# Delta net: the triangular solve by substitution on blocks of 16 rows, joined to 32 by products on quarters of the array

## The chip, the cores and the metric

The kernel runs on one core of a Trainium2 chip. It is one launch; the metric is the device time of that launch in microseconds. The engines in the profile are PE (TensorE matmuls), PEld (its weight loads), DVE (VectorE), ACT (ScalarE), POOL (GpSimd) and SP (SyncE, which here issues DMAs).

## The reference

A trunk of two layers on 1024 positions of 1024 channels. Layer 0 mixes with a gated delta net of eight heads, layer 1 with a retention; each has a convolutional FFN behind it. The change is inside the delta net. Cut to what matters:

```python
def gated_deltanet(h, w_in, conv_w, a_log, dt_bias, norm_w, w_out):
    ...
    kk = jnp.where(strict, jnp.einsum('bhncd,bhnmd->bhncm', kb, k) * decay, 0.0)
    eye = jnp.eye(C, dtype=F32)
    rhs = jnp.concatenate([v * beta[..., None], kb * jnp.exp(gc)[..., None]], axis=-1)
    sol = lax.linalg.triangular_solve(kk + eye, rhs, left_side=True, lower=True, unit_diagonal=True)
    u, w = sol[..., :dv], sol[..., dv:]
    ...
    def step(state, inp):
        q_n, k_n, u_n, w_n, qk_n, g_n = inp
        v_new = u_n - jnp.einsum('bhck,bhkv->bhcv', w_n, state)
        o = (jnp.einsum('bhck,bhkv->bhcv', q_n * jnp.exp(g_n)[..., None], state)
             + jnp.einsum('bhcm,bhmv->bhcv', qk_n, v_new))
        ...
```

Per head and chunk there is a unit lower triangular matrix, the identity plus the strictly lower part of the decayed key products. The kernel forms its inverse, here called T, and multiplies by it.

## The kernel before, in words

The kernel uses chunks of 128 positions (`P`), so eight chunks (`NCH`) for each of the eight heads (`GH`). It works on heads in pairs p = 0 to 3 and solves in two quads: `t_solve(0)` for pairs 0 and 1, `t_solve(1)` for pairs 2 and 3. The delta-net stage is one call, `run(todo)`, and stands at about 91 to 646 us of the profiled execution.

`run` interleaves generators ("streams"). Each stream has a priority, and each `yield` says after what planned delay, or after which events, it may go on. A planned clock `clk` advances by the cost given with every TensorE instruction (`pm` L630, a product; `ptr` L633, a transpose), and `pq` pins TensorE's order to the order in which the streams issue. So the planner's numbers (`cost`, the table `LAT`) fix TensorE's order; they are not the times of the chip. The order on the other engines is set by a scheduler when the kernel is built. The lowest priority belongs to `filler`: 24 items of projections for later heads and eight of the gate `z`, each of 48 products 512 wide (`acc<-hT,wh` and `acc<-hT,wl`, "fills" below). After an item, `filler` may run up to two background steps (`bg_step`, whose loads are `mvw` and whose VectorE instructions are L223 among others), but none while the list `busy` holds something.

The streams that touch the change, in the order of one pair:

- `t_front(p)`: decay factors into `U[h]` (a head's 128x128 blocks for the eight chunks), a copy of them to DRAM (`Ld`), then the key products `kk` in PSUM, multiplied into `U` (L776). The next quad's front waits for the event `Tq` of the solve before it.
- `t_solve(qd)`: copies the 32x32 diagonal blocks of 32 matrices (four heads, eight chunks) to X (L788), transposes them on VectorE to Y (L792), and builds T by 31 substitution steps: a multiply to `fs` (L800) and a subtract in T (L802), in which 128 partitions hold (block, matrix) and the free axis holds rows by columns, 31 to 256 elements. RX is T transposed back (L806); TP is a permuted copy (L808), TX its transpose (L810): both orientations of the inverted 32x32 blocks. Then `busy` is cleared and `Tq` and `T` are told.
- `t_chain(p)`: copies TX and RX to T0 and R (L838, L849, L851) and joins blocks of 32 to 64 and of 64 to 128 by small products (U on T0, the result `xa`, then `xa` and R).
- `prep(p)` (L914: values; also the keys) and `dt_half(p, q4)`: load a decay half from `Ld` to a tile DT (L941), form the scores in PSUM and multiply them into DT (L949). Both wait for `Tq`.
- `scan(p, h)`: the recurrence over the eight chunks.

SBUF tiles come from tagged pools; a new tile of a tag waits for the readers of the one whose place it takes. "lane" has four places (X, Y, T, RX, TP, TX, T0 and one DT), "t2" three. PSUM tiles of `mm` have two places, `acc` four, `sc` two.

## Time and profile before

| | |
|---|---|
| median of 3 runs | 2946.01 us (2941.49 to 2947.28) |
| the profiled execution | 2946.19 us, span 2944.4 us, mean granted TensorE clock 0.986 |
| PE, PEld, DVE, ACT, POOL busy | 96%, 78%, 75%, 45%, 20% of the span |
| delta-net stage, 91 to 646 us | 555 us: PE 520.32, DVE 384.64, ACT 302.27, POOL 120.62 us busy |

How to read the lines that follow: a group has the source line, engine, operation, out<-in by the program's names, shape and count, then busy us and mean ns of one, then idle time of the engine just before it. A row of a timeline has the start and length in us; the bracket holds the idle time ahead of it and what ended that. A window has its start and end, its length, then busy us and counts of PE, PEld, DVE, ACT and POOL, the granted clock, the DMA share and GB/s. Line numbers are those of the kernel before; in the changed kernel they move (the product is L634, the transpose L637, the substitution L813 and L816, the multiply into DT L990, the one in `prep` L955).

### The profile page before, as it was taken

The numbers are of one execution on the slowest core, as the hardware profiler recorded it, in microseconds if no ns is written. First come the engines' busy times: TensorE is split into PE (matmuls) and PEld (weight loads), VectorE is DVE, ScalarE is ACT, GpSimd is POOL, SyncE is SP. The second block draws the span as 40 slices with busy tenths as digits, with TensorE's granted clock in tenths as the row PEclk, the third lists the DMA queues.
The fourth block names the chain that finished last, engine by engine and source line by source line (L and its number), as shares of the span: only waits on it lengthen the run. The fifth ranks groups of instructions, "written<-read, shape, count | busy, mean of one in ns | idle before, by whom it ended". The sixth has DMA issues, their size and how long they took to land. (4 is left out here: it accounts for less than half of the span.)

```text
span 2944.4 us, 38880 instructions
## 1 busy us (share of the span) xinstructions
PE 2817.4 (96%) x13638; PEld 2300.7 (78%) x13638; DVE 2212.1 (75%) x3869; ACT 1317.5 (45%) x2457; POOL 580.1 (20%) x613
## 2 busy tenths in 40 slices
PE   8998999999999999999999999999999899999997
PEld 7787877887778888777787877777778688888786
DVE  5695687556788888987677766666697887778989
ACT  3655455443544444536543333221345544445443
POOL 0311220134011111520023300322201011112601
PEclk9999999999999999999999999999999999999999
DMA  8122321354344544864434454555664243335653
GB/s 300 71 79 73 104 84 50 105 181 149 111 149 159 164 157 149 306 205 139 146 119 161 157 177 153 165 172 154 197 232 152 96 136 108 108 108 197 240 179 122
DMA packets 237188, 442.36 MB, mean 150 GB/s; under 512 B 22848, under 2 KB 76352, under 8 KB 236992
## 3 DMA queue, kind: packets, MB, share of 16 engines
q1 hardware_dynamic: 206832, 387.96, 39.3%
q10 hardware_dynamic: 25152, 34.61, 3.2%
q0 software_dynamic: 5008, 17.30, 1.5%
q8 instruction: 107, 1.75, 0.2%
q14 instruction: 89, 0.73, 0.1%
HBM read 331.26 MB, written 108.53 MB: 149 GB/s over the span
## 5 line engine op out<-in xcount | busy, mean ns | idle before, releaser
L1466 PE MATMUL acc<-bb,ab 128*128 128x512 f32 x1800 | 430.5, 393 | 7.5 <-DVE bb L90 3.7
L1466 PEld LDWEIGHTS acc<-bb,ab 128*128 128x128 f32 x1800 | 338.9, 189 | 82.6 <-DVE bb L90 6.0
L630 PE MATMUL acc<-hT,wh 128*128 128x512 f32 x960 | 300.9, 395 | 0.0
L1603 POOL TENSOR_TENSOR o<-o 128x512 f32<-128x512 f32 x88 | 118.8, 1360 | 721.1 <-DVE o L1596 685.5
L1159 PE MATMUL acc<-T,wb 128*128 128x512 f32 x840 | 204.6, 393 | 7.2 <-DVE wb L90 7.2
L630 PEld LDWEIGHTS acc<-hT,wh 128*128 128x128 f32 x960 | 183.5, 191 | 34.4
L630 PE MATMUL acc<-hT,wl 128*128 128x512 f32 x480 | 203.5, 424 | 0.5 <-ACT ada L235 0.3
L89 ACT ACTIVATE ab<-ar 128x512 fp32r<-128x512 f32 x210 | 129.5, 624 | 165.2 <-PE acc L1466 89.0
L1159 PEld LDWEIGHTS acc<-T,wb 128*128 128x128 f32 x840 | 157.7, 189 | 44.3 <-DVE wb L90 11.6
L90 DVE TENSOR_TENSOR ab<-ar,ab 128x512 fp32r<-128x512 f32 x210 | 168.2, 806 | 29.6 <-ACT ab L89 29.2
L90 DVE TENSOR_TENSOR wb<-wr,wb 128x512 fp32r<-128x512 f32 x162 | 119.1, 736 | 65.7 <-ACT wb L89 65.3
L90 DVE TENSOR_TENSOR wb<-mm,wb 128x512 fp32r<-128x512 f32 x216 | 144.9, 684 | 21.5 <-ACT wb L89 19.5
L89 ACT ACTIVATE wh<-wr 128x1024 fp32r<-128x1024 f32 x101 | 107.0, 1061 | 115.0 <-PE acc L630 56.4
L90 DVE TENSOR_TENSOR wl<-wr,wh 128x1024 fp32r<-128x1024 f32 x85 | 105.2, 1237 | 66.2 <-ACT wh L89 64.0
L89 ACT ACTIVATE wb<-mm 128x512 fp32r<-128x512 f32 x216 | 122.3, 593 | 71.1 <-DVE mm L1205 70.5
L1225 ACT ACTIVATE pc<-acc 128x512 f32<-128x512 f32 x143 | 84.7, 592 | 152.7 <-PE acc L1159 99.8
L89 ACT ACTIVATE wb<-wr 128x512 fp32r<-128x512 f32 x162 | 99.4, 626 | 96.3 <-DMA wr<-in_ffn_up 53.4
L449 DVE SCALAR_TENSOR_TENSOR qkv<-raw,vc,qkv 128x512 f32<-128x512 f32 x144 | 112.2, 783 | 35.4 <-ACT qkv L447 33.2
L630 PE MATMUL acc<-wh,hT 128*128 128x512 f32 x384 | 136.0, 417 | 0.7 <-DVE vv L90 0.6
L1582 DVE SCALAR_TENSOR_TENSOR o<-g,vc,o 128x512 f32<-128x512 f32 (+2 forms) x176 | 135.3, 787 | 0.9 <-ACT o L1577 0.2
L223 DVE SCALAR_TENSOR_TENSOR ada<-mvw,e,ada 128x512 f32<-128x512 f32 x140 | 107.0, 764 | 27.3 <-DMA mvw<-in_ada_w 26.9
L110 PE MATMUL acc<-T,wb 128*128 128x512 f32 x292 | 116.7, 400 | 10.4 <-DVE wb L90 9.9
(628 smaller groups left out, 7023.9 us busy)
## 6 DMA issues: line engine op xcount, KB each, us to landing
wr<-in_ffn_up SPq DMA_DIRECT2D x96, 512.0 KB, 4.3
ad<-o SPq DMA_DIRECT2D x154, 256.0 KB, 2.3
ar<-ad SPq DMA_DIRECT2D x154, 256.0 KB, 3.8
mvw<-in_ada_w SPq DMA_DIRECT2D x48, 512.0 KB, 6.5
Br<-in_ffn_down SPq DMA_DIRECT2D x66, 256.0 KB, 3.7
mvw<-in_ada_w SPq DMA_DIRECT2D x64, 256.0 KB, 3.0
wr<-in_ret_wv SPq DMA_DIRECT2D x32, 512.0 KB, 4.1
ar<-od SPq DMA_DIRECT2D x56, 256.0 KB, 4.8
```

The lines of the kernel that those rows point to most:

```text
L89: act.activation(dst_h, src, AF.Copy)
L90: eng.tensor_tensor(dst_l, src, dst_h, ALU.subtract)
L110: mm(acc, wl[:, k], hl[0], start=first, stop=False)
L223: dve.scalar_tensor_tensor(a, wr[kk], e[:, k:k + 1], a, ALU.mult, ALU.add)
L449: dve.scalar_tensor_tensor(oh, raw[:, 3 - j:515 - j], w[:, 3 - j:4 - j], oh, ALU.mult, ALU.add)
L630: pq(pe.matmul(out, lhsT, rhs, start=start, stop=stop, **kw), cost)
L1159: return pe.matmul(*a, skip_group_check=True, **kw)
L1225: act.activation(t, X, AF.Copy)
L1466: mm_ = (lambda *a, p=p, onto=onto, **kw: (mm if p < 2 else pe.matmul)(*a, skip_group_check=onto, **kw))
L1582: dve.scalar_tensor_tensor(tv, gv[:, c0 - j:c1 - j], w[:, 2 - j:3 - j], tv, ALU.mult, ALU.add)
L1603: pool.tensor_tensor(o[d], o[x], o[y], op)
```

## The change

The substitution runs on blocks of 16 rows, two for each 32x32 block, in the same free axis: 15 steps in place of 31. Two mask columns are made at setup: m0 is 1 on the first 16 partitions of each 32, m1 on the other 16. X is folded so that each partition keeps the half of the columns that belongs to its own 16-row block. After the substitution the two inverted 16-blocks are transposed in both orientations as halves, and four masked copies put them into RX and TX as block diagonals. The off-diagonal 16-block is then made by TensorE for each matrix and each of the four 32-row blocks: `pa` is U times TX's left half, `xa` its masked copy, `pn` and `pt` are the products of `xa` with RX in the two orientations, subtracted into TX and RX. `busy.clear()` and the event `Tq` stand ahead of the joins; `T` behind them. 384 products per solve are added, 768 in all.

```diff
+    m0, m1 = mhalf[:, 4:5], mhalf[:, 5:6]
+    part = tl("sm", [P, NCH], name="part")
+    dve.tensor_reduce(part, ident.rearrange("p (x r) -> p x r", r=16), AX.X, ALU.add)
+    dve.tensor_reduce(mhalf[:, 4:6], part.rearrange("p (b s) -> p s b", s=2), AX.X, ALU.add)
...
-        Y = tl("lane", [P, 32, 32], name="Y")
-        dve.transpose(flat(Y), flat(X))
-        T = tl("lane", [P, 32, 32], name="T")
+        XY = tl("lane", [P, 2, 16, 32], name="Y")
+        act.activation(XY[:, 0], X[:, 0:16], AF.Copy, scale=m0)
+        dve.scalar_tensor_tensor(XY[:, 0], X[:, 16:32], m1, XY[:, 0], ALU.mult, ALU.add)
+        Y = XY[:, 1]
+        dve.transpose(flat(Y), flat(XY[:, 0]))
+        Y = Y.rearrange("p i (s r) -> p i s r", s=2)
+        TT = tl("lane", [P, 2, 16, 32], name="T")
+        T = TT[:, 0]
         pool.memset(T, 0.0)
-        pool.memset(flat(T)[:, 0:1024:33], 1.0)
+        for s2 in (0, 16):
+            pool.memset(flat(T)[:, s2:512:33], 1.0)
+        Tv = T.rearrange("p i (s j) -> p i s j", s=2)
         tmp = tl("fs", [P, 256], name="fs")
-        for j in range(31):
-            ni, nj = 31 - j, j + 1
-            tv = tmp[:, 0:ni * nj].rearrange("p (i j) -> p i j", j=nj)
-            dve.tensor_tensor(tv, bc(Y[:, j + 1:, j], nj), bm(T[:, j, 0:nj], ni), ALU.mult)
-            ts_ = T[:, j + 1:, 0:nj]
+        for j in range(15):
+            ni, nj = 15 - j, j + 1
+            shape = [P, ni, 2, nj]
+            tv = tmp[:, 0:2 * ni * nj].rearrange("p (i s j) -> p i s j", s=2, j=nj)
+            dve.tensor_tensor(tv, Y[:, j + 1:, :, j].unsqueeze(3).to_broadcast(shape),
+                              Tv[:, j, :, 0:nj].unsqueeze(1).to_broadcast(shape), ALU.mult)
+            ts_ = Tv[:, j + 1:, :, 0:nj]
             dve.tensor_tensor(ts_, ts_, tv, ALU.subtract)
             if j % 2:
                 yield LAT["fs"]
+        busy.clear()
+        emit(("Tq", qd_))
+        half = tl("lane", [P, 2, 16, 32], name="RTh")
+        dve.transpose(flat(half[:, 0]), flat(T))
+        act.activation(TT[:, 1].rearrange("p j (s i) -> p j s i", s=2), Tv.rearrange("p i s j -> p j s i"), AF.Copy)
+        dve.transpose(flat(half[:, 1]), flat(TT[:, 1]))
         RX = tl("lane", [P, 32, 32], name="RX")
-        dve.transpose(flat(RX), flat(T))
-        TP = tl("lane", [P, 32, 32], name="TP")
-        act.activation(TP, T.rearrange("p i j -> p j i"), AF.Copy)
         TX = tl("lane", [P, 32, 32], name="TX")
-        dve.transpose(flat(TX), flat(TP))
+        for t, c in ((RX, half[:, 0]), (TX, half[:, 1])):
+            for g, m in ((slice(0, 16), m0), (slice(16, 32), m1)):
+                act.activation(t[:, g], c, AF.Copy, scale=m)
+        xa = tl("lane", [P, 32, 32], name="xa")
+        pool.memset(xa, 0.0)
+        yield LAT["h1"]
...
+        pa = mm_tile()
+        for c, h, n in lists:
+            for bs in quads:
+                pm(pa[bs, cols(c)], U[h][bs, n, bs], TX[bs, 0:16, c], cost=0.016)
+        act.activation(xa[:, :, 0:16], pa.rearrange("p (c j) -> p c j", j=16), AF.Copy, scale=m1)
+        yield LAT["h2"]
+        pn, pt = mm_tile(), mm_tile()
+        for c, h, n in lists:
+            for bs in quads:
+                pm(pn[bs, cols(c)], RX[bs, :, c], xa[bs, c, 0:16], cost=0.016)
+        for c, h, n in lists:
+            for bs in quads:
+                pm(pt[bs, cols(c)], xa[bs, c], RX[bs, 16:32, c], cost=0.016)
+        for t, pb in ((TX[:, 0:16], pn), (RX[:, 16:32], pt)):
+            dve.tensor_tensor(t, t, pb.rearrange("p (c j) -> p j c", j=16), ALU.subtract)
         RTX[qd_] = (RX, TX)
         give("lane", 1)
-        busy.clear()
-        emit(("Tq", qd_))
         emit(("T", qd_), LAT["T"])
...
-    LAT = {... "T": 4.98, ... "fs": 2.2, ...}
+    LAT = {... "T": 2.6, ... "fs": 1.6, "h1": 5.0, "h2": 1.8, ...}
```

The change also moves work. On TensorE, from the first score product of `dt_half` at the end of solve 1 (`mm<-qkv,qkv`: scores; `mm<-cst,qkv`: transposes of `prep`; `acc<-hT`: fills), before:

```order
L630 MATMUL mm_1890<-qkv_1339,qkv_685 128x128 x4
L630 MATMUL mm_1896<-qkv_1394,qkv_686 128x128 x4
L633 MATMUL mm_1902<-cst_155,qkv_1143 128x128 x4
L633 MATMUL mm_1908<-cst_155,qkv_1703 128x128 x4
L630 MATMUL acc_1850<-hT_491,wl_1847 128x512
L630 MATMUL acc_1850<-hT_491,wh_1846 128x512 x2
L630 MATMUL mm_1917<-qkv_1479,qkv_695 128x128 x4
L630 MATMUL mm_1956<-qkv_1543,qkv_696 128x128 x4
```

And after, where the first `pa` group (TX on U) follows:

```order
L634 MATMUL mm_1682<-qkv_1342,qkv_685 128x128 x4
L634 MATMUL mm_1688<-qkv_1397,qkv_686 128x128 x4
L637 MATMUL mm_1694<-cst_155,qkv_1146 128x128 x4
L634 MATMUL acc_1610<-hT_658,wl_1565 128x512
L634 MATMUL acc_1610<-hT_658,wh_1564 128x512 x2
L634 MATMUL mm_1703<-qkv_1485,qkv_695 128x128 x4
L634 MATMUL mm_1709<-qkv_1553,qkv_696 128x128 x4
L637 MATMUL mm_1715<-cst_155,qkv_1059 128x128 x4
L634 MATMUL mm_1721<-TX_1634,U_889 32x16 x32
L634 MATMUL mm_1721<-TX_1634,U_954 32x16 x32
```

The score products stand in the same order. Between the last common pair of transposes (those of `ssq`, two groups ahead) and the first score product stand 48 + 108 + 3 = 159 fills before and 39 + 6 = 45 now: 114 fewer.

On VectorE at the end of solve 1, before:

```order
L802 TENSOR_TENSOR T_1471<-T_1471,fs_1474 128x31
L806 STREAM_TRANSPOSE RX_1862<-T_1471 128x1024
L810 STREAM_TRANSPOSE TX_1866<-TP_1864 128x1024
L949 TENSOR_TENSOR DT_1868<-DT_1868,mm_1890 128x512
L949 TENSOR_TENSOR DT_1868<-DT_1868,mm_1917 128x512
L949 TENSOR_TENSOR DT_1872<-DT_1872,mm_1956 128x512
```

And after:

```order
L990 TENSOR_TENSOR DT_1644<-DT_1644,mm_1688 128x512
...
L816 TENSOR_TENSOR T_1476<-T_1476,fs_1480 128x2x15
L822 STREAM_TRANSPOSE RTh_1629<-T_1476 128x512
L824 STREAM_TRANSPOSE RTh_1629<-T_1476 128x512
L990 TENSOR_TENSOR DT_1641<-DT_1641,mm_1682 128x512
L990 TENSOR_TENSOR DT_1641<-DT_1641,mm_1703 128x512
L990 TENSOR_TENSOR DT_1645<-DT_1645,mm_1709 128x512
```

The reader of mm_1682 stands behind the substitution and both transposes, as its like did before; it needs the load of DT_1641, which takes a lane place.

On VectorE at the end of solve 2, before (L914 readies keys and values):

```order
L802 TENSOR_TENSOR T_4014<-T_4014,fs_4017 128x31
L949 TENSOR_TENSOR DT_4401<-DT_4401,mm_4423 128x512
L806 STREAM_TRANSPOSE RX_4392<-T_4014 128x1024
L914 TENSOR_TENSOR qkv_3996<-mm_4429,ir_3671 128x512
L810 STREAM_TRANSPOSE TX_4396<-TP_4394 128x1024
L949 TENSOR_TENSOR DT_4398<-DT_4398,mm_4417 128x512
```

And after:

```order
L955 TENSOR_TENSOR qkv_4155<-mm_4445,ir_3827 128x512
L824 STREAM_TRANSPOSE RTh_4356<-T_4222 128x512
L260 TENSOR_TENSOR fh01_6897<-fh01_6897,v03_3582 128x8
L223 SCALAR_TENSOR_TENSOR ada_4422<-mvw_4424,e_162,ada_4422 128x512
L223 SCALAR_TENSOR_TENSOR ada_4422<-mvw_5008,e_162,ada_4422 128x512
L223 SCALAR_TENSOR_TENSOR ada_4422<-mvw_5009,e_162,ada_4422 128x512
L223 SCALAR_TENSOR_TENSOR ada_4422<-mvw_5269,e_162,ada_4422 128x512
L223 SCALAR_TENSOR_TENSOR ada_4422<-mvw_5270,e_162,ada_4422 128x512
L223 SCALAR_TENSOR_TENSOR ada_4422<-mvw_5426,e_162,ada_4422 128x512
L223 SCALAR_TENSOR_TENSOR ada_4422<-mvw_5427,e_162,ada_4422 128x512
L955 TENSOR_TENSOR qkv_4273<-mm_4581,ir_3945 128x512
L853 TENSOR_TENSOR TX_4361<-TX_4361,mm_4596 128x512
```

Seven L223 of a background step, with the loads of `mvw`, now stand between the last half transpose of solve 2 and its joins (L853).

More of the change, by code (lines that the diff above doesn't have):

```diff
@@ L783, in t_solve @@
         busy.append(qd_)
+        heads = pairs[2 * qd_] + pairs[2 * qd_ + 1]
         X = tl("lane", [P, 32, 32], name="X")
-        for h in pairs[2 * qd_] + pairs[2 * qd_ + 1]:
+        for h in heads:
             for b in range(4):
@@ L804, in t_solve, with cols @@
                 yield LAT["fs"]
+        busy.clear()
[4 more added lines that the diff above has]
+        dve.transpose(flat(half[:, 1]), flat(TT[:, 1]))
         RX = tl("lane", [P, 32, 32], name="RX")
-        dve.transpose(flat(RX), flat(T))
-        TP = tl("lane", [P, 32, 32], name="TP")
-        act.activation(TP, T.rearrange("p i j -> p j i"), AF.Copy)
         TX = tl("lane", [P, 32, 32], name="TX")
-        dve.transpose(flat(TX), flat(TP))
+        for t, c in ((RX, half[:, 0]), (TX, half[:, 1])):
[4 more added lines that the diff above has]
+        yield LAT["h1"]
+        quads = [slice(32 * b, 32 * b + 32) for b in range(4)]
+        lists = [(h % 4 * 8 + n, h, n) for h in heads for n in range(NCH)]
+        def cols(c):
+            return slice(16 * c, 16 * c + 16)
+        pa = mm_tile()
[13 more added lines that the diff above has]
+            dve.tensor_tensor(t, t, pb.rearrange("p (c j) -> p j c", j=16), ALU.subtract)
         RTX[qd_] = (RX, TX)
         give("lane", 1)
-        busy.clear()
-        emit(("Tq", qd_))
         emit(("T", qd_), LAT["T"])
@@ L1092, in filler @@
                 owed[0] -= 1
-    LAT = {"kk": 3.05, "ld": 1.14, "g1": 17.30, "gm": 2.50, "mm": 1.81, "T": 4.98, "X": 3.38, "fs": 2.2, "T0": 5.00, "t1": 1.65, "t2": 2.35, "t3": 1.34, "D": 2.67, "s1": 1.60, "s2": 1.22, "s3": 1.26, "tail": 12.31, "ssq": 9.30, "fv": 2.85}
+    LAT = {"kk": 3.05, "ld": 1.14, "g1": 17.30, "gm": 2.50, "mm": 1.81, "T": 2.6, "X": 3.38, "fs": 1.6, "h1": 5.0, "h2": 1.8, "T0": 5.00, "t1": 1.65, "t2": 2.35, "t3": 1.34, "D": 2.67, "s1": 1.60, "s2": 1.22, "s3": 1.26, "tail": 12.31, "ssq": 9.30, "fv": 2.85}
     pairs = [(2 * p, 2 * p + 1) for p in range(GH // 2)]
```

## The prediction

> **What bounds the kernel now.** I read the page's busy shares first, then the windows of the delta-net stage (91 to 646 us; only it is touched), the waits of TensorE in it, and the timelines at its stalls. The page:

> ```profile
> PE 2817.4 (96%) x13638; PEld 2300.7 (78%) x13638; DVE 2212.1 (75%) x3869; ACT 1317.5 (45%) x2457; POOL 580.1 (20%) x613
> ```

> TensorE is busy 96% of the span. The windows (start:end, length; then busy us and count of PE, PEld, DVE, ACT, POOL; granted clock, DMA share, GB/s):

> ```profile
> 143.00:174.00 31.00, 31.00 (x163) 26.37 (x162) 27.50 (x110) 24.54 (x42) 6.91 (x10) 1.00 0.19 65
> 174.00:216.00 42.00, 41.45 (x195) 34.22 (x194) 39.17 (x83) 21.30 (x59) 0.94 (x7) 1.00 0.23 79
> 216.00:236.00 20.00, 11.76 (x65) 10.17 (x66) 13.40 (x29) 12.52 (x29) 5.25 (x15) 0.83 0.15 52
> 385.00:412.00 27.00, 20.58 (x107) 16.80 (x106) 23.82 (x103) 16.89 (x30) 8.49 (x13) 0.89 0.39 136
> 412.00:478.00 66.00, 65.41 (x313) 54.62 (x312) 58.20 (x144) 35.03 (x80) 5.70 (x14) 1.00 0.15 54
> 478.00:486.00 8.00, 4.87 (x28) 4.21 (x29) 5.18 (x7) 7.82 (x16) 5.25 (x14) 0.89 0.33 122
> 560.00:646.00 86.00, 86.00 (x558) 75.92 (x559) 47.20 (x111) 36.19 (x83) 18.61 (x13) 0.98 0.44 154
> ```

> The substitutions run in 174:216 and 412:478. There TensorE is full (41.45 of 42, 65.41 of 66) with the filler's projections, while VectorE is nearly full too. And 560:646 is 86.00 of 86.00: the stage ends in projections that fill every gap. So a projection pulled forward into a hole shortens the tail, one pushed back lengthens it, and the stage's time is TensorE's work plus its waits. A shorter substitution by itself buys nothing; it counts only through the waits. These are (us in total, times, longest):

> ```profile
> PE mm L630 <- DVE DT L949: 8.1, 2, 5.6
> PE mm L630 <- DVE U L776: 4.1, 1, 4.1
> PE acc L327 <- DVE hl L90: 2.8, 1, 2.8
> ```

> The stalls sit at the end of solve 1 (216:236: 8.2 us idle and, at a clock of 0.83, 3.4 us lost to speed: 11.6), at the end of solve 2 (478:486: 3.1 + 0.9 = 4.0) and in the `kk` products of pairs 2 and 3 (385:412: 6.4 + 3.0 = 9.4).

> **Part 1: 768 small products (+13.0).** Each solve adds three groups of 128 products on 32x16 or 32x32 quarters. The nearest rows are the 32x32 joins of `t_chain` (a group by form: count, then busy us; and two rows of one pair's `pb`; each fp32 product leaves two records):

> ```profile
> L630 PE MATMUL mm<-T,U 32*32 32x32 f32 x256 | 8.4, 192 | 0.0
> 242.38 0.21 PE L630 MATMUL mm<-R,xa 32*32 32x32 f32 x1
> 243.41 1.08 PE L630 MATMUL mm<-R,xa 32*32 32x32 f32 x29
> ```

> T,U: 128 products, each on the same quarter of the array as the one before it, in 8.4 us: 66 ns each. From 242.38 to 243.41 R,xa and xa,R alternate between two column quarters, 32 products in 1.03 us: 32 ns; the 16 that follow sit on one quarter again and take 1.08. The new groups go round four diagonal quarters. Two quarters halved the time, so I take four to quarter it: 16 ns, an estimate. 768 x 0.016 = 12.3 us, plus six group changes of 0.1 to 0.2 us, 0.7. Ends: 6.5 if the 16-wide operand halves it once more, and 51 at 66 ns.

> The rows show two column quarters of one PSUM bank written together; none shows two row quarters doing so. [...]

> **Part 2: the substitution on VectorE (0 by itself).** Rows:

> ```profile
> L802 DVE TENSOR_TENSOR T<-T,fs 128x31 f32<-128x31 f32 (+15 forms) x62 | 21.1, 340 | 1.2
> L800 DVE TENSOR_TENSOR fs<-Y,T 128x31 f32<-128x31 f32 (+15 forms) x62 | 21.1, 340 | 1.1
> 435.55 0.25 DVE L800 TENSOR_TENSOR fs<-Y,T 128x87 f32<-128x87 f32 x1
> ```

> 42.2 us become 60 instructions of 30 to 128 elements, on average 91, so 60 x 0.25 = 15 us: 27 us fall off VectorE. The 1024-wide transposes (1.25 us each) become three halves, and a 0.75 us fold is added. ScalarE's added masks (about 5 us a solve) and GpSimd's memset lie beside a full TensorE except at the solve's end, below. [...]

> **Part 3: the end of solve 1 (+1.7).** Here is what stands there before:

> ```profile
> 173.30 1.25 DVE L792 STREAM_TRANSPOSE Y<-X 128x1024 f32<-128x1024 f32 x1 [0.44 <-ACT X L788]
> 216.96 2.05 PE L630 MATMUL mm<-qkv 128*128 128x128 f32 x16 [1.51 <-DVE qkv L914]
> 219.80 0.66 PE L633 MATMUL mm<-cst,qkv 128*128 128x128 f32 x4 [0.79 <-DVE DT L949]
> 221.30 0.66 PE L633 MATMUL mm<-cst,qkv 128*128 128x128 f32 x4 [0.85 <-DVE qkv L914]
> 223.84 1.96 ACT L808 ACTIVATE TP<-T 128x1024 f32<-128x1024 f32 x1 [5.01 <-DVE T L802]
> 228.71 1.42 DVE L949 TENSOR_TENSOR DT<-DT,mm 128x512 f32<-128x512 f32 x2 [1.63 <-DMA DT<-Ld]
> 229.45 2.08 PE L630 MATMUL mm<-qkv 128*128 128x128 f32 x8 [5.56 <-DVE DT L949]
> 398.45 1.06 PE L630 MATMUL mm<-qkv 128*128 128x128 f32 x8
> ...
> 168.83 0.39 PE L630 MATMUL acc<-hT,wh 128*128 128x512 f32 x1
> 169.06 0.39 PE L630 MATMUL acc<-hT,wl 128*128 128x512 f32 x1
> 169.28 0.62 PE L630 MATMUL acc<-hT,wh 128*128 128x512 f32 x2
> 169.74 0.39 PE L630 MATMUL acc<-hT,wl 128*128 128x512 f32 x1
> ```

> TensorE reaches the score products of `dt_half`, and waits 1.51 + 0.79 + 0.85 + 5.56 = 8.7 us. The last is a chain: T ready 223.8, `TP` copied to 225.8, the load of `DT` (it takes a lane buffer that `TP`'s reader frees) lands 2.9 us later at 228.7, and the multiply releases a PSUM buffer. Afterwards eight records take 2.08 us in place of 1.06 (the row at 398.45): half speed.

> After the change, Tq comes ahead of the joins, and in the new order 114 fewer projections stand ahead of the first score product. At 0.227 us each (three from 169.06 to 169.74) TensorE gets there 25.8 us sooner than 216.96 - 1.51 = 215.45, at 189.6, and is past the first two scores (1.06 us) near 190.9. VectorE begins at 173.3 with the fold (0.6 + 0.75) and half transpose (0.65), then 30 substitution steps with their gaps (8.7), and by the new order 7 of L449 (0.746), 3 of L223 (0.75, and their loads some 1.6), one L90 (1.2), two L955, one L990 (0.69 each) and two small ones: 12.4 in all, so T is ready near 197. Half transposes and the masks of L829 (0.65 + 0.6 + 0.65 + half of 2.4) put TX at 200.4. The load for DT_1641 now waits for RTh's readers, the masks, so it lands 2.9 later, 203.3; its multiply releases mm_1709 at 204, where TensorE arrives near 195.9. `mm` has two PSUM buffers; mm_1682 holds one, and mm_1694 and mm_1703 each wait for the reader of the other, an L990 and an L955 among the substitution's rows, 2.4 us. With the 8.1 for mm_1709 that is 10.5 against 8.7, with the same half-speed stretch. **+1.7**; between -8.7 (the load finds its buffer early) and +5 (VectorE 3 us later).

> **Part 4: the end of solve 2 (+5.5).** Before:

> ```profile
> L449 DVE SCALAR_TENSOR_TENSOR qkv<-raw,vc,qkv 128x512 f32<-128x512 f32 x28 | 20.9, 746 | 1.6 <-ACT qkv L447 1.5
> 423.99 1.05 PE L630 MATMUL mm<-qkv 128*128 128x128 f32 x8
> 482.89 1.49 DVE L949 TENSOR_TENSOR DT<-DT,mm 128x512 f32<-128x512 f32 x2 [1.62 <-DMA DT<-Ld]
> 483.64 1.50 PE L630 MATMUL mm<-qkv 128*128 128x128 f32 x8 [2.56 <-DVE DT L949]
> ```

> Count from the last `kk` product (423.99). The new order puts 114 projections and a few transposes ahead of the first `pa` product, so TensorE is there after 28.7 us. VectorE starts the solve after 8.5 us and has in its order, up to the second half transpose (L824), 7.5 + 0.9 us of substitution, 17 of L449, and L90 and L955 rows: 24.4 us, so it ends at 33.0 and TX follows at 33.6. TensorE waits 5 us and then pays a half-speed stretch of 2.6 (five us at half speed, as after 407 and 229). Next, `pt` needs a PSUM buffer whose reader (L955 on mm_4581) stands behind seven L223 and their three successive loads; at some 3.7 us a pair that ends at 45.2, with `pn` done at 43: 2 more. 9.6 against 4.0, **+5.5**; between -4 (no wait) and +9.

> **Part 5: the `kk` stage (-6.5).** The `busy` list now empties earlier in solve 1 and later background steps are taken elsewhere: the new order has no L223 between the `kk` products of pairs 2 and 3. Before:

> ```profile
> L223 DVE SCALAR_TENSOR_TENSOR ada<-mvw,e,ada 128x512 f32<-128x512 f32 x5 | 3.7, 747 | 0.4 <-DMA mvw<-in_ada_w 0.4
> 407.29 2.08 PE L630 MATMUL mm<-qkv 128*128 128x128 f32 x8 [4.10 <-DVE U L776]
> ```

> VectorE is 23.82 of 27 busy there and TensorE waits for its L776. With 3.7 us less ahead, most of the 4.1 us wait and its half-speed stretch (2.6) go: -6.5 of the 9.4. Ends: 0 and -9.4.

> **Part 6: the stage's end (-1.5).** The tail now ends in more projections, so the first product behind it (L327) may find its operand ready: half of 2.8. What the scans wait for (Sn L985 and the like) keeps its order: 0, +-3. The two reductions at setup: 0, hidden by TensorE's first projections; 0.5 if not.

> **Sum.** +13.0 + 1.7 + 5.5 - 6.5 - 1.5 = +12.2 on the profiled execution's 2946.19 (span 2944.4 and 1.8 outside it), 0.2 above the median of 2946.01: 2958.

> **Rivals.**

> *A, the four quarters run in series.* 66 ns each: 768 x 0.066 = 50.7 in place of 12.3, +38.4: 2997. For it: nothing shown has two row quarters at work in one bank. Against: column quarters of one bank do overlap. 10 in 100.

> *B, only two quarters overlap.* 32 ns as in the R,xa row: +12.3, 2971. For it: it is the only overlap the trace has. 13 in 100.

> *C, faster: VectorE, 27 us lighter, is ahead of TensorE at both solves.* Its place is the PSUM and lane buffers at mm_1709 and TX at `pa`: if DT's load is out before TensorE's 195.9, and TX ready before 28.7, the waits of Parts 3 and 4 vanish with their slow stretches (-11.6 and -4.0) and Parts 1 and 5 leave +6.5: less Part 6, 13.0 - 11.6 - 4.0 - 6.5 - 1.5 = -10.6, 2935. It decides at 5 us on VectorE in solve 2 and 8 in solve 1. For it: VectorE's lighter load is the larger number. Against: the orders keep VectorE at the solve's end full with L449, and the chain of masks and load is longer, not shorter. 17 in 100.

> *D, no change.* Solve 2's joins find TX ready (-9.6 on my sum): 2949. 17 in 100.

> **Numbers.** Mine has the remaining 43; its own range is 2952 to 2966. 0.2% (5.9 us) is about what a measurement can tell from no change. Slower: mine, A and B, 66; same: D, 17; faster: C, 17. The range of 2936 to 2974 leaves out A and half of C.

> **What would show it.** Each of the six groups `pa`, `pn`, `pt` is about 2 us wide (A: 8.4; B: 4.1). TensorE's waits list an 8 us one on L990 near 204 and a 5 us one on TX (ACT L829) in solve 2, then one on L955 behind L223. 385:412 loses under 4 us. L813 and L816 sum to about 15 us. I am wrong if the groups are wider than 3 us each, or if the two stalls at the solves are shorter than those before.

## The result, and the profile after

The changed kernel takes 2988.36 us (median of 4 runs, 2984.91 to 2989.87) against 2943.75 us for the kernel before on the same chip: a ratio of 1.0147, 95% interval 1.0134 to 1.0159. It is slower by 43 us by the ratio (44.6 between the two medians), where +12 was forecast with 2974 as the upper end. The profiled execution took 2987.05 us (span 2985.3).

The page of the changed kernel, busy shares and one line of its DMA queues, and behind it the same DMA line of the kernel before:

```profile
PE 2843.7 (95%) x15174; PEld 2325.4 (78%) x15174; DVE 2175.2 (73%) x3813; ACT 1325.5 (44%) x2471; POOL 582.0 (19%) x617
q8 instruction: 119, 1.95, 0.3%
```

```profile
q8 instruction: 107, 1.75, 0.2%
```

TensorE has 1536 more matmuls, two for each of the 768 products, and as many more weight loads: 3072 instructions. VectorE has lost 37 us. The second line counts a queue of loads that neither kernel issues, the instructions themselves: packets, MB, share of the DMA engines. 12 more packets came, 0.0164 MB each, one for each 256 of the added instructions.

The windows of the changed kernel, at the stretches shown of the kernel before and at two more:

```profile
143.00:174.00 31.00, 31.00 (x164) 26.32 (x162) 28.47 (x110) 23.76 (x42) 6.41 (x9) 1.00 0.26 86
174.00:216.00 42.00, 30.16 (x588) 25.56 (x589) 25.28 (x59) 16.10 (x50) 2.10 (x4) 0.84 0.19 54
216.00:236.00 20.00, 17.11 (x412) 14.59 (x407) 2.87 (x4) 10.55 (x20) 5.71 (x16) 0.74 0.06 23
236.00:300.00 64.00, 56.73 (x415) 47.41 (x412) 38.18 (x81) 30.56 (x78) 5.02 (x12) 0.89 0.21 67
385.00:412.00 27.00, 25.11 (x132) 20.59 (x131) 24.60 (x68) 18.31 (x27) 13.72 (x16) 1.00 0.36 125
412.00:478.00 66.00, 53.41 (x879) 45.31 (x880) 48.69 (x155) 30.55 (x52) 7.30 (x12) 0.88 0.23 73
478.00:486.00 8.00, 8.00 (x146) 7.38 (x143) 0.69 (x1) 6.17 (x13) 5.50 (x15) 0.69 0.02 4
```

Look at the clock column: 0.84, 0.74, 0.89, 0.88, 0.69 around both solves. Before, 174:216, 236:300 and 412:478 stood at 1.00, and 216:236 and 478:486 at 0.83 and 0.89. In 478:486 TensorE is busy throughout and still at two thirds of its speed. From the first solve on the stage runs some 14 us later than before, so 385:412 now holds only the first part of the `kk` products; Part 5 below comes back to that.

To divide the loss I took windows of 1 us from 91 us to the stage's end (the first product of L327, at 649.36 before and 693.87 after): idle is their length less PE's busy time, the loss to speed is busy time times one minus the clock. Idle went from 37.5 to 52.2 us (+14.7), the loss to speed from 12.3 to 27.9 (+15.6), and the rest of the 44.5 us, 14.2, is work. (The split between the last two is rough: the burst of `pt` at 218.16, shown below, ran at 0.50 and took 1.90 of the 3.46 us to the next one, so the low clock there need not have cost time.) Of the waits of TensorE in the stage after the change, these bear on the argument:

```profile
PE mm L634 <- issue: 10.7, 6, 2.7
PE mm L634 <- DVE DT L990: 8.4, 2, 8.0
PE mm L634 <- ACT TX L829: 4.4, 1, 4.4
PE mm L634 <- DVE R L923: 3.3, 1, 3.3
```

The second and third were forecast. The first was not: "issue" is time in which TensorE waited for nothing that the profile shows, and all six cases are inside the new groups. The timeline at the end of solve 1:

```profile
199.65 2.08 PE L634 MATMUL mm<-qkv 128*128 128x128 f32 x8 [7.97 <-DVE DT L990]
201.52 1.06 PE L637 MATMUL mm<-cst,qkv 128*128 128x128 f32 x4
202.60 1.56 PE L634 MATMUL mm<-TX,U 32*32 32x16 f32 x149
206.43 1.67 PE L634 MATMUL mm<-TX,U 32*32 32x16 f32 x107 [2.26 <-issue]
...
212.92 3.82 PE L634 MATMUL mm<-xa,RX 32*32 32x16 f32 x256
216.58 0.25 PE L634 MATMUL mm<-RX,xa 32*32 32x16 f32 x8
218.16 1.90 PE L634 MATMUL mm<-RX,xa 32*32 32x16 f32 x128 [1.34 <-issue]
221.62 1.80 PE L634 MATMUL mm<-RX,xa 32*32 32x16 f32 x120 [1.55 <-issue]
```

`pa` breaks off after 149 records, `pt` runs in a burst of exactly 128 and waits again. 128 matmuls and their 128 weight loads are 256 instructions, and 218.16 to 221.62 is 3.46 us. At 17 ns a product (measured in e1 below) the 64 products of such a burst would be done in 1.1 us.

The queue of instructions shows the supply itself. Here is the DMA rate of the changed kernel from 200 to 225 us, in 40 slices of 0.625 us, and the count of that queue's packets:

```profile
GB/s 0 0 0 0 0 0 26 0 0 0 0 0 26 0 0 0 0 0 26 0 0 0 0 0 105 170 334 223 26 7 26 0 0 0 0 0 26 0 0 0
q8 instruction: 6, 0.10, 1.7%
```

The values of 26 in the slices from 203.75, 207.5, 211.25, 218.75 and 222.5 are one packet of 16 KB each; a sixth, at 215.46, lies under another load. Those that start at 203.79, 215.46 and 219.20 land at 205.00, 216.64 and 220.20, and the bursts at 206.43, 218.16 and 221.62 begin 1.4 to 1.5 us behind them. It is the same at all 49 holes of this run and of the five runs in the table below that have holes: each ends 1.1 to 1.6 us after such a packet has landed. While TensorE waits for them, packets come one by one, here 3.7 to 4.2 us apart.

### The profile page after: what moved, and what is told of

It is laid out like the page before. It is cut to its first block, busy times and chain, and to the rows that moved or that the text cites. A ratio compares the mean times of both kernels' runs of the same rounds, so it can differ in the third digit from the quotient of the medians.

```text
span 2985.3 us, 41888 instructions
## 1 busy us (share of the span) xinstructions
PE 2843.7 (95%) x15174; PEld 2325.4 (78%) x15174; DVE 2175.2 (73%) x3813; ACT 1325.5 (44%) x2471; POOL 582.0 (19%) x617
## 5 line engine op out<-in xcount | busy, mean ns | idle before, releaser
L1200 PEld LDWEIGHTS acc<-T,wb 128*128 128x128 f32 x840 | 159.1, 190 | 43.9 <-DVE wb L90 10.7
L90 DVE TENSOR_TENSOR ab<-ar,ab 128x512 fp32r<-128x512 f32 x210 | 168.2, 807 | 30.3 <-ACT ab L89 30.2
L90 DVE TENSOR_TENSOR wb<-wr,wb 128x512 fp32r<-128x512 f32 x162 | 119.2, 737 | 66.2 <-ACT wb L89 64.6
L90 DVE TENSOR_TENSOR wb<-mm,wb 128x512 fp32r<-128x512 f32 x216 | 145.1, 685 | 20.9 <-ACT wb L89 19.0
L90 DVE TENSOR_TENSOR wl<-wr,wh 128x1024 fp32r<-128x1024 f32 x85 | 105.4, 1240 | 69.8 <-ACT wh L89 69.8
L449 DVE SCALAR_TENSOR_TENSOR qkv<-raw,vc,qkv 128x512 f32<-128x512 f32 x144 | 113.0, 789 | 50.5 <-ACT qkv L447 46.1
L89 ACT ACTIVATE wb<-wr 128x512 fp32r<-128x512 f32 x162 | 99.8, 627 | 91.9 <-DMA wr<-in_ffn_up 50.7
L223 DVE SCALAR_TENSOR_TENSOR ada<-mvw,e,ada 128x512 f32<-128x512 f32 x140 | 105.6, 754 | 28.4 <-DMA mvw<-in_ada_w 28.3
```

Source lines behind the costliest of these rows:

```text
L89: act.activation(dst_h, src, AF.Copy)
L90: eng.tensor_tensor(dst_l, src, dst_h, ALU.subtract)
L223: dve.scalar_tensor_tensor(a, wr[kk], e[:, k:k + 1], a, ALU.mult, ALU.add)
L449: dve.scalar_tensor_tensor(oh, raw[:, 3 - j:515 - j], w[:, 3 - j:4 - j], oh, ALU.mult, ALU.add)
L1200: return pe.matmul(*a, skip_group_check=True, **kw)
```

## The experiments

Theory S: the groups of 128 products outrun the supply of instructions; the holes, and the low use of the array in and around them, put TensorE at half speed. (In its strict form the holes alone do that.) Rival W: the loss lies in the waits on DT, TX and R that the early `Tq` brought. All ratios are to the kernel before on the same chip; "holes" are the waits put down to "issue".

| run | us | ratio (95%) | holes | idle | lost to speed |
|---|---|---|---|---|---|
| before | 2943.75 to 2947.79 | 1 | 0 | 37.5 | 12.3 |
| after | 2988.36 | 1.0147 (1.0134 to 1.0159) | 10.7 | 52.2 | 27.9 |
| e1 joins by head, fills between | 2963.46 | 1.0055 (1.0039 to 1.0070) | none | 36.5 | 14.2 |
| e9 joins by head, no fills between | 2981.26 | 1.0120 (1.0103 to 1.0137) | 12.5 | 47.5 | 25.2 |
| e4 no products | 2945.09 | 0.9996 (0.9986 to 1.0005) | none | 36.5 | 11.9 |
| e2 before + products | 2980.81 | 1.0114 (1.0097 to 1.0131) | 16.0 | 48.0 | 28.3 |
| e3 late `Tq` | 2982.45 | 1.0120 (1.0105 to 1.0135) | 13.6 | 51.2 | 25.9 |
| e5 before + one-pass products | 2964.57 | 1.0059 (1.0046 to 1.0073) | 8.9 | 42.4 | 21.9 |
| e6 the same, twice | 2981.42 | 1.0119 (1.0104 to 1.0135) | 22.7 | 57.0 | 27.6 |

(Holes, idle and loss to speed from 91 us to 690 or 694, of the profiled execution. It took 2940.22 us in e4, 2974.51 in e9 and 2986.20 in e2, some 5 to 7 us from the median of those runs.)

**e4: without the products.**

```diff
-        pa = mm_tile()
...
-            dve.tensor_tensor(t, t, pb.rearrange("p (c j) -> p j c", j=16), ALU.subtract)
+        yield LAT["h2"]
```

> The changed kernel without the pa, pn and pt products, their evacuation and the two subtractions: the off-diagonal 16-blocks are left out of T. All else stays. Theory S: 11.6 us own time, 10.7 us holes and some 8 to 12 us of half speed go: 2954 to 2960 us. Rival W: own time alone goes, 2974 to 2978.

2945.09, below theory S's 2954 to 2960. All that the change costs hangs on the products; and all that it saves on VectorE, with everything else that it moves, is worth nothing: 0.9996.

**e2: the products alone, added to the kernel before.**

```diff
         emit(("T", qd_), LAT["T"])
+        yield 5.0
+        pa = mm_tile()
+        for c, h, n in lists:
+            for bs in quads:
+                pm(pa[bs, 16 * c:16 * c + 16], U[h][bs, n, bs], TX[bs, 0:16, c], cost=0.016)
+        yield 1.8
...
```

> The kernel before, with the 768 quarter products added behind each solve in groups of 128 on RX and TX and U, their results not used; nothing else is changed. Theory S: own time 11.6 us, plus holes of 8 to 11 and half speed of 6 to 10: 2970 to 2978 us. Rival W: own time alone, 2956 to 2960.

2980.81, 35.6 us above the 2945.25 beside it, a little more than S expected. With nothing moved ahead, the holes (16.0 us) and the slow stretches are there all the same, so W falls for the most part.

**e1: the joins cut by head, with fills between the groups.**

```diff
-        pa = mm_tile()
-        for c, h, n in lists:
+        for h in heads:
+            c0 = h % 4 * 8
+            pa = mm_tile()
+            for n in range(NCH):
...
+            yield 1.4
```

(`pn` and `pt` of a head share one tile and end in `yield 2.4`.)

> The changed kernel with its joins cut by head: four groups of 32 pa products and four of 64 pn and pt products, each with its own evacuation, and 9 to 15 fills between groups. Same products. Theory S (the groups of 128 outrun the instruction supply, about 256 instructions in 3.4 us, and the holes and the thin groups put TensorE at half speed): the waits put down to 'issue' fall from 10.7 us to under 2 and the time lost to half speed from 27.9 us to about 17: 2966 to 2972 us. Rival W (the loss is in the waits on DT L990, TX L829 and R L923, which early Tq brought): nothing of that changes, 2986 to 2992.

2963.46, 3 us better than S's range: the same products, 25 us off. Its waits at the solves are nearly those of the changed kernel (7.3 us on DT, 3.4 on TX). The same window of e1 and of the changed kernel, both behind the DT stall:

```profile
212.00:240.00 28.00, 28.00 (x734) 22.93 (x733) 11.21 (x21) 15.73 (x30) 5.88 (x18) 1.00 0.14 40
```

```profile
212.00:240.00 28.00, 25.11 (x714) 21.25 (x712) 6.68 (x10) 14.86 (x28) 5.71 (x16) 0.80 0.08 22
```

Busy 28.00 at 1.00 against 25.11 at 0.80.

**e9: the same cut, no fills between.**

```diff
-            yield 1.4
+            yield 0.0
...
-            yield 2.4
+            yield 0.0
```

> e1 without the planned delays between its groups: the joins cut by head with the same small evacuations, but the groups one after another with no fills between them. Theory S (the fills between are what cures): holes put down to 'issue' are back at 8 us or more and the time at 2980 to 2992. Rival C (the cut by head cures, by smaller PSUM groups and earlier evacuation): 2960 to 2968 as e1.

2981.26, and 12.5 us of holes: it is the fills between that cure, not the cut.

**e5 and e6: how many instructions, or how much work.** 768 one-pass bfloat16 products on constants (two instructions each in place of four), once and twice per group, behind each solve of the kernel before.

```diff
+            for _ in range(1):      # e6: range(2)
+                for c in range(32):
+                    for bs in quads:
+                        pm(t[bs, 16 * c:16 * c + 16], db[bs, 0:32], db[bs, 32:48], cost=0.016)
```

> The kernel before with the same 768 quarter products added at the same places as in e2, but on bfloat16 constants, so that each is one weight load and one matmul in place of two of each: half the instructions per group, no use made of the results. Theory S (256 instructions in some 3.4 us is what the engine is supplied with): a group of 256 instructions runs out of the store once at most, 'issue' waits of TensorE fall from e2's 16.0 us to under 4, half speed stays near before's 12 us: 2950 to 2960. Rival P (the four quarters disturb one another in one PSUM bank, or thin products by themselves bring half speed): holes and slow stretches stay, 2968 or more.

> As e5, but each group has its 128 products twice, so it has as many instructions as e2's group of 128 fp32 products. Theory S: the holes come back as in e2 (10 us or more put down to 'issue') with their slow stretches, 2970 to 2985. Rival P: own time only twice that of e5, no holes, 2960 to 2968.

e6 has e2's count of instructions and takes e2's time, 2981.42 against 2980.81, though its products are other ones. The holes are back (22.7 us). e5 has half and takes half of the excess, but its holes fell only to 8.9 us where I expected under 4; 2964.57 is 5 us above S's range. At solve 1 the first group, 256 instructions by itself, has no hole; the holes come where the second group, the third and the next small joins follow one another. The timeline of e6 behind solve 1:

```profile
241.62 1.84 PE L631 MATMUL mm<-cst 32*32 32x16 bf16 x207
245.99 1.21 PE L631 MATMUL mm<-cst 32*32 32x16 bf16 x128 [2.52 <-issue]
249.71 1.19 PE L631 MATMUL mm<-cst 32*32 32x16 bf16 x128 [2.52 <-issue]
253.44 0.53 PE L631 MATMUL mm<-cst 32*32 32x16 bf16 x48 [2.53 <-issue]
```

The bursts are 128 matmuls, and begin 3.72 and 3.73 us apart. The packets of the instruction queue grow with the count of added instructions too: 107 before, 113 in e5, 119 in e6 and e2. That is one packet for each 256 added instructions (1536 in e5, 3072 in e6 and e2), as many as a burst has with its weight loads. With wide products between the groups (e1) no hole is left.

**e3: `Tq` and `busy.clear()` back behind the joins.**

```diff
-        busy.clear()
-        emit(("Tq", qd_))
         half = tl("lane", [P, 2, 16, 32], name="RTh")
...
         give("lane", 1)
+        busy.clear()
+        emit(("Tq", qd_))
```

> The changed kernel with busy.clear() and the event Tq put back behind the joins. Theory S: the groups and their holes stay; without the score products TensorE has only fills while the solve ends, so the stall on L990 moves and the time stays within 10 us, 2978 to 2992. Rival W: the stalls of early Tq (8.0 and 4.4 us with their slow stretches) go, 2962 to 2972.

2982.45, as S expected: TensorE then waits more for TX (9.6 us in two waits) and less for DT (5.0).

**e13: why `pn` is dearer.** In e1, at full speed, 64 records of `pa` or `pt` take 0.55 us from first start to last (17 ns a product), those of `pn` 0.93 (29 ns).

```diff
-                    pm(pb[bs, cols(n)], RX[bs, :, c0 + n], xa[bs, c0 + n, 0:16], cost=0.016)
+                    pm(pb[bs, cols(n)], xa[bs, c0 + n], xa[bs, c0 + n, 0:16], cost=0.016)
```

> e1 with another weight operand in the pn products: a matrix's xa, whose 32 columns lie side by side, in place of RX, whose columns lie 32 elements apart; shapes and count are the same, and the off-diagonal block in T's one orientation is left wrong. If the spacing of the weights is why pn takes 29 ns a product in e1 where pa and pt take 17: the group of 64 records falls from 0.93 to 0.55 us between starts and the kernel by 2 to 3 us, 2959 to 2962. If it is the place of the product (first in its group, behind a wide fill): 29 ns stays, 2961 to 2966.

The timeline of e1, two groups that follow each other, then that of e13:

```profile
223.89 1.10 PE L634 MATMUL mm<-xa,RX 32*32 32x16 f32 x64
224.82 0.72 PE L634 MATMUL mm<-RX,xa 32*32 32x16 f32 x64
```

```profile
221.97 0.69 PE L634 MATMUL mm<-xa 32*32 32x16 f32 x62
222.50 0.18 PE L634 MATMUL mm<-RX,xa 32*32 32x16 f32 x1
```

From the first group's start to the second's it is 0.93 in e1 and 0.53 in e13: the spaced weights cost 12 ns a product, 3 us in all. The kernel's time, 2963.35 at a ratio of 1.0055 (1.0036 to 1.0073), doesn't resolve it.

**e14 and e15: what brings half speed.** One run each, of thin work that is never short of instructions: 32 one-pass products 512 wide on one quarter, or on four quarters in turn, behind each solve of the kernel before.

```diff
+        for _ in range(32):
+            pm(t[0:32], db[0:32, 0:32], db[0:32, 128:640], cost=0.216)
```

```diff
+        for _ in range(32):
+            for bs in quads:
+                pm(t[bs], db[bs, 0:32], db[bs, 128:640], cost=0.054)
```

> The kernel before with 32 products on one 32x32 quarter of the array added behind each solve, one pass on constants and 512 wide, so some 7 us of unbroken work in 64 instructions. Their results are not used. No instruction is short here. If thin work by itself brings half speed (rival T), the granted clock falls to 0.5 within the group or just behind it. If the holes bring it (theory S in its strict form), the clock stays at 1.00 through the group and the kernel takes 14 us more than before.

> As e14 with each product made on all four diagonal quarters in turn, 128 products of 512 columns. If the quarters overlap as in the joins, the group takes little longer than e14's 7 us. Rival T: half speed as in e14, or less of it with four quarters at work; theory S in its strict form: 1.00 throughout.

e14 took 2967.73 and e15 2948.82 us, beside 2947.16 for the kernel before; these are single runs, and the clock is what is read from them. Windows of e14 inside its first group (one quarter alone from 230.15 to 242.08), then of e15 around its first (from 231.33; the last product starts at 238.79):

```profile
231.00:232.00 1.00, 1.00 (x4) 0.42 (x3) 0.00 (x0) 0.98 (x2) 0.00 (x0) 0.50 0.00 0
233.00:234.00 1.00, 1.00 (x4) 0.33 (x3) 0.00 (x0) 0.00 (x0) 0.00 (x0) 0.50 0.00 0
237.00:238.00 1.00, 1.00 (x4) 0.39 (x3) 0.00 (x0) 0.00 (x0) 0.00 (x0) 0.50 0.00 0
```

```profile
229.00:232.00 3.00, 3.00 (x20) 2.28 (x22) 1.63 (x3) 2.90 (x7) 1.08 (x5) 0.50 0.00 0
232.00:234.00 2.00, 2.00 (x32) 0.79 (x28) 0.13 (x1) 1.89 (x3) 0.00 (x0) 0.78 0.04 8
234.00:238.00 4.00, 4.00 (x80) 1.81 (x76) 0.00 (x0) 0.00 (x0) 0.00 (x0) 1.00 0.00 0
```

Both groups start at 0.50, behind the wait for DT. In e14 TensorE is busy without a break for 12 us and the clock stays at 0.50; in e15 it is back at 1.00 at 232.89, 1.6 us into the group. The second groups, e14's then e15's:

```profile
486.00:488.00 2.00, 1.76 (x7) 0.69 (x7) 1.45 (x3) 0.00 (x0) 0.00 (x0) 0.86 0.48 142
488.00:496.00 8.00, 8.00 (x20) 2.68 (x19) 1.51 (x2) 0.00 (x0) 0.00 (x0) 0.50 0.32 96
```

```profile
480.00:481.00 1.00, 1.00 (x15) 0.39 (x8) 0.74 (x1) 0.00 (x0) 0.00 (x0) 0.50 0.45 170
483.00:484.00 1.00, 1.00 (x28) 0.53 (x20) 0.00 (x0) 0.00 (x0) 0.00 (x0) 1.00 0.57 193
```

Each starts at 1.00 behind an idle gap (1.92 us in e14, 2.02 in e15), and in both the clock falls to 0.50 about 1 us into the group (at 487.42 and 478.65). So the fall can't be put down to the single quarter: e15 falls as well. What differs is what follows: e15 is back at 1.00 after 3.4 us, e14 stays at 0.50 for 17 us, to the end of its group and through the joins behind it.

So theory S in its strict form falls: in e14 TensorE stays at 0.50 for 12 us without a hole. What differs between the two runs is how much of the array works. With one quarter, kept busy, the clock did not come back (12 and 17 us at 0.50); with four quarters and wide products it did (after 1.6 and 3.4 us). The joins go round four quarters too, but only 16 columns wide. At the end of 3.7 us of `pn` the clock of the changed kernel falls to 0.50 (at 216.65), ahead of the hole and with no gap in the 3.4 us at 1.00 before it (213.24 to 216.65):

```profile
214.00:215.00 1.00, 1.00 (x85) 1.00 (x80) 1.00 (x2) 0.00 (x0) 0.00 (x0) 1.00 0.00 0
215.00:216.00 1.00, 1.00 (x84) 1.00 (x80) 0.08 (x1) 0.63 (x1) 0.00 (x0) 1.00 0.77 123
217.00:218.00 1.00, 0.00 (x0) 0.00 (x0) 0.50 (x1) 0.00 (x0) 0.00 (x0) 0.50 0.28 107
```

How full the array has to be for full speed no run measures, nor how the lost time divides between the holes and the thin work.

**Versions that might beat both.** Four runs move TensorE's plan at the solves, one quiets the `kk` stage. They are retunings of one number or one list.

```diff
-        yield LAT["ld"]      # e7 in before, e8 in e1
+        yield 12.0 if q4 == 0 and p % 2 == 0 else LAT["ld"]
...
-"fs": 2.2      # e10: before; e11: e1, 1.6 to 2.4
+"fs": 2.8
...
+        if p > 1:      # e12: before, in t_front ahead of kk, taken off again behind it
+            busy.append(("kk", p))
```

> The kernel before with the planned delay from the load of DT to its score product raised from 1.14 to 12 us for the first half of pairs 0 and 2, so that fills stand ahead of that product. No product is added or left out. Theory S: the waits on DT L949 (8.1 us) and the slow stretch behind them shrink, 2936 to 2943. Rival W': VectorE is late in any case and the stall moves to the next product: 2944 to 2949.

> e1 (joins cut by head with fills between) with the same delay of 12 us as in e7. Theory S: of e1's waits the 7.3 us on DT and 4.9 us of half speed behind it go, 2951 to 2957. Rival W': the stall moves to the next product, 2960 to 2966.

> The kernel before with the planner's delay per two substitution steps raised from 2.2 to 2.8, so that 36 more fills stand ahead of the end of solve 1 and some ahead of that of solve 2; no work is changed. If the stall there is only a plan that runs ahead of VectorE, its 8.7 us and the slow stretch shrink: 2934 to 2941. Rival: fills put there are missing later, or VectorE gets more work from them and ends as much later: 2943 to 2950.

> e1 with the planner's delay per two substitution steps raised from 1.6 to 2.4, 18 or so more fills ahead of the end of solve 1. If the stall on DT and TX is a plan that runs ahead, 7 to 10 us less than e1: 2953 to 2957. Rival, as in e10: 2960 to 2966.

> The kernel before with the background steps held back while the kk products of pairs 2 and 3 are made, which the change did as a side effect (8.8 us lost there before, 1.9 after). If those steps are what VectorE is late with: 385 to 412 loses under 3 us and the kernel takes 2937 to 2942. Rival: the steps are only put off and cost as much elsewhere: 2943 to 2948.

e7: 2957.45, 1.0040 (1.0028 to 1.0052); its runs spread over 22 us, and the profile is of the fastest, so it does not explain the median. e8: 2958.54, 1.0037 (1.0025 to 1.0050): the DT wait went and TX took its place (L829, 12.2 us in two waits). e10: 2955.66, 1.0026 (1.0016 to 1.0037). e11: 2963.14, 1.0054 (1.0040 to 1.0067), no change to e1, as its rival said. e12: 2950.25, 1.0010 (1.0001 to 1.0020): 385:412 still lost 6.6 us, and 478:486 lost 7.2 us of idle where before it was 3.1. e7, e10 and e12 lie above both of their ranges, e8 between its two. In e8, e10 and e12 the stall came back elsewhere. None beats the kernel before; e8 has the lowest time of the forms of the change (its interval overlaps e1's), and is slower.

## Why the prediction was wrong, point by point

**Part 1 failed, and it is the whole miss.** The term was +13.0, "four quarters in turn, 16 ns". The overlap is there: 17 ns for `pa` and `pt` and, for the spaced weights, 29 for `pn`: 256 x (17 + 17 + 29) = 16.1 us. (The 0.7 for group changes was my own estimate, and the trace shows no such pause where `pt` follows `pn`: from 212.92 to 216.58 are 3.66 us, 28.6 ns for each of the 128 products, no more than the 29 of e1.) But I priced TensorE's pace only: what feeds it, and the clock that it runs at, stood at nothing in the sum, without a reason. The runs put 10.7 us of holes on top, and over the whole stage 15.6 us more lost to half speed. With fills between the groups (e1) the holes are gone and the loss to speed is 14.2 us where it was 12.3 before, and the kernel takes 18 us more than before, close to the 16.1. The rows to see it in were there: the joins that I took the price from come in groups of 16 to 48 products with other products around them, and a group of 128 never occurs. Without the products (e4) the change takes what the kernel before takes, so the other parts leave nothing of the 43 us. They summed to -0.8, but that this agrees is partly luck: e4 still waits longer for DT (10.6 us for 8.1) and gets it back elsewhere, among others at L327.

**Four quarters in one PSUM bank**, where rival A has its doubt, did not cost time here. In e14 a product on one quarter follows the one before by 0.215 us at full speed (0.427 at half); in e15 four products, one on each quarter and all into one PSUM tile, start together every 0.216 us at full speed: four at four times the pace of one. Rival A ended at 2997, near the result, but the series of 66 ns a product that it stands on is not there (17 and 29 ns): that it came so close is luck. Rival B's overlap of two quarters (32 ns) is not there either.

**Part 2 was right.** The groups of the changed kernel:

```profile
L816 DVE TENSOR_TENSOR T<-T,fs 128x30 f32<-128x30 f32 (+7 forms) x30 | 7.6, 253 | 0.7
L813 DVE TENSOR_TENSOR fs<-Y,T 128x30 f32<-128x30 f32 (+7 forms) x30 | 7.6, 252 | 0.6
```

15.2 us against 15 forecast, and by itself worth 0 (e4).

**Part 3** was right in kind: a wait of 7.97 us on DT where 8.1 stood, with 1.50 in place of 2.4 ahead of it. The size is partly luck. TensorE came to the wait at 191.68, not 195.9, and it ended at 199.65, not 204: two errors of some 4 us cancel. (The terms given for VectorE add to 196.4 where I wrote 197; T was ready at 192.4.) In waits the part was +0.8, not +1.7. The half-speed stretch behind the wait ended at 203.0; a second one, from 206.4 to 213.2, began at the end of the hole in `pa`.

**Part 4** was right for TX (4.4 for 5): TensorE came to `pa` 28.7 us behind the last `kk` product, as forecast. The sum behind it was not right, since 7.5, 0.9 and 17 alone are over the 24.4 written for them with L90 and L955 besides. The wait of `pt` behind L223 did not come: the reader L955 ended at 470.5, and `pn`, held up by the hole of 2.74 us in `pa`, only at 472.7.

**Part 5** was right in kind and too large. The window 385:412 lost 8.8 us before and 1.9 after, but it does not hold the same work: the `kk` products stand at 385 to 425 before and at 399.6 to 426.2 after. Over these stretches 9.1 us were lost before and 4.5 after, so 4.6 went where 6.5 was forecast. The wait for VectorE's multiply into U is still there (2.62 us at 416.08), but no half-speed stretch follows it (1.00 up to 458.9). e12 made part of the same edit alone: it lost 2.2 us less at `kk`, 4.1 more of idle in 478:486, and gained nothing. In this one case a wait that went was found again at the next point where VectorE is late.

**Part 6**: L327 no longer waits. The scans' waits (`sc`) went from 4.9 to 8.0 us, the edge of the +-3. One wait that I had not on the list is in the joins of `t_chain`: R L923, 3.3 us, with half speed from about 247 to 261. e1 and e4 don't have that slow stretch.

**The losses before** were read too large in two places: "lost to speed" of 3.4 (216:236) and 3.0 us (385:412) counts idle time as well; by busy time alone, in windows of 1 us, it is 2.8 and 2.4. Rival C used the first.

## What to carry to other kernels

Price many small products by three things: their pace on the array (here 17 or 29 ns), their instructions against what the engine is supplied with (here 256 in 3.5 to 3.7 us), and the clock while little of the array works (0.50 in e14). Put wide products between groups of small ones: the same 768 products cost 43 us in groups of 128 and 18 us in groups of 32 or 64, mostly with 9 or 12 fills between. And try the relief of an engine in a run of its own first, without the work that pays for it (e4): where another engine is full to the end, 27 us less substitution on VectorE was worth nothing.
